# Two transformer blocks on one core: junctions, gates and the end of a recurrence rewritten together

## The chip, the cores and the metric

The kernel runs on one NeuronCore of a Trainium2 chip. The metric is the device time of one execution in microseconds; the kernel before has a median of 2291.05 us over three runs (2288.86 to 2294.74).

## What is computed

256 tokens of width 1024 go through a first block of two layers and a second block. Cut from the reference:

```
def first_block(x, ...):
    for layer in range(2):
        if layer == 0: mix = _diff_attention(x, ...)
        else:          mix = _stick_breaking(x, ...)          # keys and values from x too
        x = _layer_norm(ALPHA * x + mix, ln_g[layer, 0], ln_b[layer, 0])
        ffn = _peer(x, w_q, sub_keys, u, v)     # top 16 of 128 x 128 experts, 8 heads
        x = _layer_norm(ALPHA * x + ffn, ln_g[layer, 1], ln_b[layer, 1])

def rg_lru(x, w_a, b_a, w_i, b_i, lam):
    r = sigmoid(block_diag_linear(x, w_a, b_a))
    i = sigmoid(block_diag_linear(x, w_i, b_i))
    log_a = -8 * r * softplus(-lam)
    a = exp(log_a)
    bx = sqrt(-expm1(2 * log_a)) * (i * x)
    h = scan: h_t = a_t * h_(t-1) + bx_t

def second_block(x, ...):
    u = rms_norm(x, attn_pre_norm)
    q, k, v, x_lru, g_lru, gate_attn, gate_lru = split(u @ w_in)
    y_attn = moba_attention(q, k, v) @ w_branch_attn
    y_lru  = (rg_lru(conv(x_lru)) * gelu(g_lru)) @ w_branch_lru
    mix = (sigmoid(gate_attn) * y_attn + sigmoid(gate_lru) * y_lru) @ w_out
    h = x + rms_norm(mix, attn_post_norm)
    m = square(relu(rms_norm(h, mlp_pre_norm) @ w_up)) @ w_down
    return h + rms_norm(m, mlp_post_norm)
```

## The kernel before

The tokens lie in two halves of 128, b = 0 and b = 1. Every projection is done in split precision: a weight tile `raw` (128x1024) is cut by ScalarE into `hi` (`Stream.split`, L66) and by VectorE into `lo` = `raw` − `hi` (L67); so are the activations into `xh` and `xl` (`part`, L163 and L164); and three products hi·hi, lo·hi and hi·lo are added in a PSUM bank (`mm3`, L157 to L159, or `mm_n`, L182). All weights of the program pass through one `Stream` in the order of use. `next()` hands out a tile, issues the loads of the tiles three ahead on SP's queue, and cuts two ahead, or `extra` more; the cuts of the tiles named by `keep` go into buffers of their own. Each engine runs its instructions in the order in which the Python code issues them, so the place of a call in the code is its place in the engine's queue.

A stage ends in a *junction*: the last projection (`proj_n`, or the loop over the 128 row tiles of experts in `peer`) adds into four banks `ps_acc`, two for each half of the tokens. The products of the last `DEFER` = 6 tiles for b = 1 are held back (`held`), so that TensorE has them to do while the norm of b = 0 runs on VectorE and ScalarE. Then `layer_norm` norms b = 0 (`norm`, tiles `lny`, `lnm`, `lnr`, result `x` or `xr`), transposes it (`transposed`, bank `ps_m`, L289), multiplies it by the first `NJ` = 4 tiles of the next stage (`half_pass(0)`), and does the same for b = 1 (`half_pass(1)`). `half_pass(0)` takes its four tiles with `next()`, so the cuts that `next()` issues stand in the midst of it.

Block 2 norms by the root of the mean square. In `post_norm` ScalarE squares the banks with a sum (`msj`, `mss`, L910), VectorE scales (`qnu`) and adds to `x` (L944); `pre_norm` squares `x` again, scales by a gain (`pnu`) and by the root (L927, L928). Its mixer works on eight column tiles at a time: projections `gl`, `ga`, `gg` are copied from PSUM, `rr` and `ii` are Sigmoids of the block-diagonal products (L1163), and `ga` and `gl` are made Sigmoids later, 512 columns at a time (L1166). A generator in the background (`bg.tick()`) issues the attention heads and the recurrence: exponent `rr` times `decay`, `aa`, the factor under the root, the scans over `xc`, the Gelu of `gg`.

The tile `x` is spilled to DRAM (`xs`) between stages and read again when the next norm needs it.

## Time and profile before

| | |
|---|---|
| median of three runs | 2291.05 us (2288.86 to 2294.74) |
| profiled execution | 2293.14 us |
| its span in the profile | 2291.4 us |
| granted TensorE clock, mean | 0.991 |
| busy: TensorE, VectorE, ScalarE, GpSimd | 2224.8, 1744.0, 1238.1, 35.6 us |
| HBM | 437.39 MB read, 39.85 MB written |

The span is what the profile's rows cover; the profiled execution's own time is 1.7 us longer, and 2.1 us over the median. PE is TensorE, PEld its weight loads, DVE VectorE, ACT ScalarE, POOL GpSimd, SP SyncE; SPq and POOLq are DMA issues of these queues.

### The profile page before, as it was taken

What the parts mean: (1) busy time and instruction counts of PE and PEld (TensorE: products, weight loads), DVE (VectorE), ACT (ScalarE), POOL (GpSimd) and SP (SyncE); (2) the same over time, 40 slices, a digit from 0 to 9 for tenths busy, and PEclk for the clock granted to TensorE, in tenths of its full rate; (3) what the DMA queues carried; (4) which work ended last, traced back from release to release, by engine and by line L of the source; (5) the groups of instructions that cost most, each with busy time, mean ns of one, the idle gap of its engine ahead of it and who ended that gap; (6) DMA issues with size and microseconds to landing.
All of it is one profiled execution on the core that took longest, in us unless ns stands there. A gap on an engine that the chain in (4) does not pass through costs nothing.

```text
span 2291.4 us, 39855 instructions
## 1 busy us (share of the span) xinstructions
PE 2224.8 (97%) x15028; PEld 2007.0 (88%) x15028; DVE 1744.0 (76%) x3496; ACT 1238.1 (54%) x2128; POOL 35.6 (2%) x81
## 2 busy tenths in 40 slices
PE   8999999999999999999999999999999899998998
PEld 7779999999888887988999999888888689997987
DVE  6869999887666668577998988766667757676654
ACT  5644455666444444674445566544445447754543
POOL 4100000000000000000000000000000000000000
PEclk9999999999999999999999999999999999999999
DMA  7446676556777776554667665777877574464664
GB/s 251 153 171 229 217 239 222 199 197 234 241 243 260 241 243 215 170 169 166 230 225 235 211 205 190 244 243 240 262 240 254 171 214 141 145 215 154 204 192 140
DMA packets 152706, 481.96 MB, mean 210 GB/s; under 512 B 18752, under 2 KB 19648, under 8 KB 151232
## 3 DMA queue, kind: packets, MB, share of 16 engines
q1 hardware_dynamic: 131456, 442.69, 59.9%
q10 hardware_dynamic: 19008, 34.61, 4.0%
q8 instruction: 118, 1.93, 0.3%
q0 software_dynamic: 2048, 2.10, 0.3%
q14 instruction: 76, 0.62, 0.1%
HBM read 437.39 MB, written 39.85 MB: 208 GB/s over the span
## 4 chain that ended last, share of the span: by engine, by line
PE 87%; DVE 5%; ACT 4%; DMA 2%; issue 2%; POOL 0%; SPq 0%; DVEq 0%; ACTq 0%
PE ps_acc L182 35%; PE ps_h L157 15%; PE ps_h L159 15%; PE ps_h L158 14%; DVE lo L67 2%; PE ps_acc L807 1%; PE ps_acc L808 1%; ACT hi L66 1%; PE ps_acc L158 1%; PE ps_acc L157 1%; PE ps_acc L159 1%; DMA raw<-w_up 1%; PE ps_acc L691 0%; PE ps_m L289 0%; DVE lns L308 0%
## 5 line engine op out<-in xcount | busy, mean ns | idle before, releaser
L67 DVE TENSOR_TENSOR lo<-raw,hi 128x1024 fp32r<-128x1024 f32 x740 | 902.3, 1222 | 444.2 <-ACT hi L66 441.4
L66 ACT CAST hi<-raw 128x1024 fp32r<-128x1024 f32 x740 | 775.1, 1050 | 434.1 <-issue 308.5
L157 PE MATMUL ps_h<-xh,hi 128*128 128x256 f32 x2784 | 789.3, 284 | 3.7 <-ACT r L1239 2.2
L159 PE MATMUL ps_h<-xh,lo 128*128 128x256 f32 x2784 | 774.2, 278 | 1.5 <-DVE lo L67 1.4
L158 PE MATMUL ps_h<-xl,hi 128*128 128x256 f32 x2784 | 773.9, 278 | 0.0
L157 PEld LDWEIGHTS ps_h<-xh,hi 128*128 128x128 f32 x2784 | 525.9, 189 | 9.0 <-ACT r L1239 2.5
L159 PEld LDWEIGHTS ps_h<-xh,lo 128*128 128x128 f32 x2784 | 523.9, 188 | 2.8 <-DVE lo L67 2.5
L158 PEld LDWEIGHTS ps_h<-xl,hi 128*128 128x128 f32 x2784 | 524.4, 188 | 0.2
L182 PE MATMUL ps_acc<-hi,wh 128*128 128x512 f32 x1024 | 315.6, 389 | 3.3 <-ACT wh L163 3.3
L182 PE MATMUL ps_acc<-lo,wh 128*128 128x512 f32 x1024 | 315.2, 389 | 0.0
L182 PE MATMUL ps_acc<-hi,wo 128*128 128x512 f32 x1024 | 315.2, 389 | 0.0
L834 ACT ACTIVATE hs<-ps_h 128x256 f32<-128x256 f32 x256 | 98.3, 384 | 343.4 <-PE ps_h L159 173.0
L182 PEld LDWEIGHTS ps_acc<-hi,wh 128*128 128x128 f32 x1024 | 192.0, 188 | 43.5 <-ACT wh L163 3.6
L182 PEld LDWEIGHTS ps_acc<-lo,wh 128*128 128x128 f32 x1024 | 192.2, 188 | 40.0
L182 PEld LDWEIGHTS ps_acc<-hi,wo 128*128 128x128 f32 x1024 | 192.2, 188 | 39.8
L164 DVE TENSOR_TENSOR wo<-jd,wh 128x256 fp32r<-128x256 f32 x256 | 107.2, 419 | 2.0 <-ACT wh L163 2.0
L858 DVE TENSOR_TENSOR jd<-G,jd 128x256 f32<-128x256 f32 x256 | 107.0, 418 | 2.2 <-ACT G L810 2.2
L163 ACT CAST wh<-jd 128x256 fp32r<-128x256 f32 x256 | 101.7, 397 | 10.1 <-DVE jd L858 10.1
L810 ACT ACTIVATE G<-ps_acc 128x64 f32<-128x64 f32 (+1 forms) x256 | 82.1, 384 | 6.7 <-PE ps_acc L808 1.0
L157 PE MATMUL ps_h<-hi,xh 128*128 128x512 f32 x160 | 70.3, 439 | 13.1 <-ACT hi L66 11.0
L158 PE MATMUL ps_h<-lo,xh 128*128 128x512 f32 x160 | 68.3, 427 | 5.7 <-DVE lo L67 5.7
L159 PE MATMUL ps_h<-hi,xl 128*128 128x512 f32 x160 | 67.8, 423 | 2.0 <-DVE xl L164 2.0
(326 smaller groups left out, 2349.7 us busy)
## 6 DMA issues: line engine op xcount, KB each, us to landing
raw<-peer_u SPq DMA_DIRECT2D x256, 512.0 KB, 4.5
raw<-peer_v SPq DMA_DIRECT2D x256, 512.0 KB, 4.0
H<-hs SPq DMA_DIRECT2D x128, 256.0 KB, 2.1
jd<-H ACTq DMA_DIRECT2D x128, 256.0 KB, 3.9
raw<-w_in SPq DMA_DIRECT2D x32, 512.0 KB, 3.7
raw<-w_up SPq DMA_DIRECT2D x32, 512.0 KB, 3.8
raw<-w_down SPq DMA_DIRECT2D x32, 512.0 KB, 3.7
raw<-w_qkv SPq DMA_DIRECT2D x24, 512.0 KB, 4.5
```

What stands on the lines that cost most here:

```text
L66: self.nc.scalar.copy(hi, raw)
L67: self.nc.vector.tensor_sub(lo, raw, hi)
L157: mm(out, lh, rh, start=start, stop=False)
L158: mm(out, lh, rl, start=False, stop=False)
L159: mm(out, ll, rh, start=False, stop=stop)
L163: self.nc.scalar.copy(hi, src)
L164: self.nc.vector.tensor_sub(lo, src, hi)
L182: mm(acc[half], x, w[:, half * 512 : half * 512 + 512], start=a, stop=b)
L807: mm(out, o[:, 0, j], o[:, 1, j], start=True, stop=False)
L810: nc.scalar.activation(gt[:, :, 4 * g : 4 * g + 4], ps.rearrange("p (t i) -> p i t", t=4)[:, first:end], AF.Copy, scale=1.0 / GSCALE,)
L834: nc.scalar.activation(hs[i // 2][:, i % 2], o, AF.Gelu)
L858: nc.vector.tensor_tensor(w, g[:, i - first], hl[i // 2][:, i % 2], ALU.mult)
```

## The change

Seven edits come together. TensorE's list of products is as long as before; the order of some held products changes.

1. *Cuts.* `half_pass(0)` calls `next(calm=True)`, which cuts nothing ahead; the cuts that stood there are issued in `half_pass(1)`. All four junction tiles are cut before the norm: in `peer` by `extra` in the last iterations (two cuts more, at i = 119 and 120), elsewhere by a `split` ahead of `half_pass(0)`.
2. *Held products* run as half 0 (512 columns) of all six jobs and then half 1 (`finish`).
3. *`norm`:* the centring of the second 512 columns stands behind `x` of the first.
4. *Norms around the MLP:* `pre_norm` is left out. `u` = `x` · gain is formed at once for each 512 columns, and the root, which scales a row as a whole, is computed behind `half_pass(1)` (`late_norm`), squared into `factor`, and used in the last `post_norm`.
5. *35 DMAs* (spills, reloads, gains, masks, tables) are issued by POOL in place of SP.
6. *Gates:* `ga` and `gl` become Tanh at the copy from PSUM, `ii` Tanh, `rr` Exp; a sigmoid is (1 + tanh(z/2))/2 or 1/(1 + exp(−z)), the one folded into the operations behind it, the other by four VectorE RECIPROCALs of 128x512. Four activation table loads go, one is added; ScalarE has 2174 rows for 2183, VectorE 3155 for 3128.
7. *The recurrence's end* is issued in ten steps of one scan each, without the wait for all eight `gg`.

```
@@ class Stream
-    def next(self):
+    def next(self, calm=False):
-        self.split(i + 1 + self.split_ahead + self.extra, i)
+        self.split(i + 1 if calm else i + 1 + self.split_ahead + self.extra, i)
@@ finish, proj_n, half_pass
+    def finish(self, held):
+        for half in range(2):
+            for job in held:
+                self.mm_n(*job, (half,))
-            self.st.extra = max(0, min(2, NJ * (k + 2 - count + defer) // defer))
+            self.st.extra = max(0, min(2, k - count + 6))
-                tiles.append(self.st.next())
+                tiles.append(self.st.next(calm=True))
+            elif j:
+                self.st.split(self.st.used + j, self.st.used)
@@ norm
-        for s in halves:
-            nc.vector.scalar_tensor_tensor(y[:, s], y[:, s], mv[:, 0:1], g[:, s], ALU.subtract, ALU.mult)
+        centre = lambda s: nc.vector.scalar_tensor_tensor(y[:, s], y[:, s], mv[:, 0:1], g[:, s], ALU.subtract, ALU.mult)
+        centre(halves[0])
         next(root)
         for s in halves:
+            if s is halves[1]:
+                centre(s)
             nc.vector.scalar_tensor_tensor(x[:, b, s], y[:, s], r, beta[:, s], ALU.mult, ALU.add)
@@ layer_norm
+        self.st.split(self.st.used + NJ, self.st.used)
         next(n1)
         self.half_pass(0, tiles)
@@ peer
-                    nc.sync.dma_start(xr, spill)
+                    nc.gpsimd.dma_start(xr, spill)
+                if i >= GSPLIT:
+                    self.st.extra = min(2, (i - GSPLIT) // 4)
                 hi, lo = self.st.next()
@@ late_norm, post_norm
+    def late_norm(self, pool, x, square):
+        r = pool.tile([P, 1], F32, tag="lt_r", name=f"ltr{self.n}", bufs=2)
+        yield from self.mean_square(pool, r, [x[:, :512], x[:, 512:]], 1e-6)
+        self.nc.vector.tensor_tensor(square, r, r, ALU.mult)
             if out is not None:
                 nc.sync.dma_start(out[:, s], x[:, s])
+            if then:
+                then(s)
@@ block2, recurrence
+                nc.vector.reciprocal(decay, decay)
-                            nc.vector.tensor_scalar(rr[i][:, j], rr[i][:, j], d, None, ALU.mult)
+                            nc.vector.tensor_scalar(rr[i][:, j], rr[i][:, j], 1.0, d, ALU.add, ALU.mult)
+                        nc.vector.reciprocal(rr[i], rr[i])
-                while len(gelus) < KD:
-                    yield
-                for i in range(4 + 2):
+                for step in range(10):
+                    i, odd = divmod(step, 2)
...
+                            while len(gelus) < 2 * i + 2:
+                                yield
@@ block2, gates
-                        project(dst, c)
+                        nc.scalar.activation(dst[:, c], self.proj_t(self.xh, self.xl), AF.Tanh, scale=0.5)
-                nc.scalar.preload_act_table(AF.Sigmoid)
-                            nc.scalar.activation(d, o, AF.Sigmoid, bias=cv[:, c, 5 + i : 6 + i])
-                for g in (ga, gl):
-                    for c in range(half * 4, half * 4 + 4, 2):
-                        nc.scalar.activation(g[:, c : c + 2], g[:, c : c + 2], AF.Sigmoid)
+                            if dst is rr:
+                                nc.scalar.activation(d, o, AF.Exp, scale=-1.0, bias=gb[:, c, 0:1])
+                            else:
+                                nc.scalar.activation(d, o, AF.Tanh, scale=0.5, bias=gb[:, c, 1:2])
-                nc.vector.tensor_tensor(ya[:, c], o, ga[:, c], ALU.mult)
+                nc.vector.scalar_tensor_tensor(ya[:, c], ga[:, c], 1.0, o, ALU.add, ALU.mult)
@@ block2, junction
-                self.post_norm(two, acc[b], x[:, b], gains[0])
-                u = self.pre_norm(two, x[:, b], gains[1])
+                u = two.tile([P, D], F32, tag="ln_y", name=f"lnu{b}", bufs=2)
+                scaled = lambda s: nc.vector.tensor_tensor(u[:, s], x[:, b, s], gains[1][:, s], ALU.mult)
+                self.post_norm(two, acc[b], x[:, b], gains[0], then=scaled)
             self.half_pass(1, tiles)
-            nc.sync.dma_start(spill, x)
+            for b in range(NB):
+                for _ in self.late_norm(two, x[:, b], factor[:, b : b + 1]):
+                    pass
+            nc.gpsimd.dma_start(spill, x)
@@ MLP
-            nc.sync.dma_start(x, spill)
+            nc.gpsimd.dma_start(x, spill)
-                self.post_norm(two, acc[b], x[:, b], gain, a["out"][b * P : b * P + P])
+                self.post_norm(two, acc[b], x[:, b], gain, a["out"][b * P : b * P + P], factor[:, b : b + 1])
```

VectorE at peer 0's junction, the end of the norm of b = 1 (`lny`, `lnr`, `xr`) up to the split of its transposed values (`xl`), before:

```order
L264 TENSOR_TENSOR lnr_10685<-rsy_10706,rsz_10707 128x1
L316 SCALAR_TENSOR_TENSOR xr_9153<-lny_10682,lnr_10685,gains_10290 128x512 x2
L67 TENSOR_TENSOR lo_10722<-raw_10608,hi_10721 128x1024
L67 TENSOR_TENSOR lo_10734<-raw_10719,hi_10733 128x1024
L67 TENSOR_TENSOR lo_10746<-raw_10731,hi_10745 128x1024
L67 TENSOR_TENSOR lo_10758<-raw_10743,hi_10757 128x1024
L164 TENSOR_TENSOR xl<-ps_m_10767,xh 128x4x128
L164 TENSOR_TENSOR xl<-ps_m_10774,xh 128x4x128
```

The same place after the change:

```order
L273 TENSOR_TENSOR lnr_10695<-rsy_10716,rsz_10717 128x1
L329 SCALAR_TENSOR_TENSOR xr_9153<-lny_10692,lnr_10695,gains_10290 128x512
L323 SCALAR_TENSOR_TENSOR lny_10692<-lny_10692,lnm_10694,gains_10290 128x512
L329 SCALAR_TENSOR_TENSOR xr_9153<-lny_10692,lnr_10695,gains_10290 128x512
L164 TENSOR_TENSOR xl<-ps_m_10759,xh 128x4x128
L164 TENSOR_TENSOR xl<-ps_m_10766,xh 128x4x128
L67 TENSOR_TENSOR lo_10781<-raw_10735,hi_10780 128x1024
L67 TENSOR_TENSOR lo_10791<-raw_10743,hi_10790 128x1024
L67 TENSOR_TENSOR lo_10801<-raw_10751,hi_10800 128x1024
```

The four cuts `lo` stood between the norm and `xl`; now three stand behind `xl`, and the junction's other two are among the rows of the loop.

ScalarE at the junction behind the mixer, from the transposed values of b = 0 (`xh`) to those of b = 1, before:

```order
L163 CAST xh<-ps_m_24260 128x4x128
L163 CAST xh<-ps_m_24267 128x4x128
L66 CAST hi_24291<-raw_24281 128x1024
L66 CAST hi_24303<-raw_24289 128x1024
L910 ACTIVATE msj_24315,mss_24316<-ps_acc_24064 128x512
L910 ACTIVATE msj_24315,mss_24316<-ps_acc_24065 128x512
L258 ACTIVATE rsy_24323<-mss_24316,eps1e-06_76 128x1
L259 ACTIVATE rsy_24323<-rsy_24323 128x1
L910 ACTIVATE msj_24335,mss_24336<-x_23763 128x512 x2
L258 ACTIVATE rsy_24342<-mss_24336,eps1e-06_76 128x1
L259 ACTIVATE rsy_24342<-rsy_24342 128x1
L928 ACTIVATE pnu_24334<-pnu_24334,pnr_24333 128x512
```

The same place after the change:

```order
L163 CAST xh<-ps_m_24245 128x4x128
L163 CAST xh<-ps_m_24252 128x4x128
L927 ACTIVATE msj_24293,mss_24294<-ps_acc_24066 128x512
L927 ACTIVATE msj_24293,mss_24294<-ps_acc_24067 128x512
L266 ACTIVATE rsy_24301<-mss_24294,eps1e-06_76 128x1
L267 ACTIVATE rsy_24301<-rsy_24301 128x1
L163 CAST xh<-ps_m_24313 128x4x128
L163 CAST xh<-ps_m_24320 128x4x128
```

The two `hi` ahead of the Squares of b = 1 and the second root are gone from between the two transpositions.

VectorE in the mixer around the second pair of `rr` (exponents of the recurrence; `su` and `p` belong to an attention head), before:

```order
L164 TENSOR_TENSOR cl_22549<-xc_21398,ch_22548 128x256
L1076 TENSOR_SCALAR rr_21389<-rr_21389,decay_21912 128x256 x2
L1081 TENSOR_TENSOR ii_21397<-ii_21397,xc_21398 128x512
L1039 RECIPROCAL su_22541<-su_22541 128x2
L1041 TENSOR_SCALAR p_22539<-p_22539,su_22541 128x128
```

The same place after the change:

```order
L164 TENSOR_TENSOR cl_22553<-xc_21406,ch_22552 128x256
L1108 TENSOR_SCALAR rr_21397<-rr_21397,decay_21919 128x256 x2
L1109 RECIPROCAL rr_21397<-rr_21397 128x512
L1114 SCALAR_TENSOR_TENSOR ii_21405<-ii_21405,xc_21406 128x512
L1070 RECIPROCAL su_22545<-su_22545 128x2
L1072 TENSOR_SCALAR p_22543<-p_22543,su_22545 128x128
```

A RECIPROCAL of 512 columns stands ahead of the head's `su` and `p`.

## Rows read from the trace of the kernel before

**Rows 1.** The page's first part, busy time, share of the span and instructions of each engine, and a line of its fourth part, the share of each engine in the chain of work that ended last.

```profile
PE 2224.8 (97%) x15028; PEld 2007.0 (88%) x15028; DVE 1744.0 (76%) x3496; ACT 1238.1 (54%) x2128; POOL 35.6 (2%) x81
...
PE 87%; DVE 5%; ACT 4%; DMA 2%; issue 2%; POOL 0%; SPq 0%; DVEq 0%; ACTq 0%
```

**Rows 2.** Windows over the whole span; of each stretch from:to (us) its length, then busy time (and instructions) of each engine, then the granted TensorE clock, the busy share of the DMA engines, and GB/s. The stretches are the ends of layer 0, peer 0, peer 1, the mixer of block 2, and the kernel.

```profile
99.00:145.00 46.00, 40.79 (x172) 31.00 (x170) 34.54 (x62) 24.34 (x49) 0.00 (x0) 0.94 0.37 126
...
904.00:922.00 18.00, 13.65 (x48) 10.05 (x48) 11.73 (x19) 5.84 (x9) 0.00 (x0) 0.81 0.40 125
...
1782.00:1835.00 53.00, 45.56 (x187) 35.31 (x187) 39.66 (x76) 25.71 (x45) 0.14 (x2) 0.94 0.44 149
...
2066.00:2110.00 44.00, 36.16 (x145) 28.19 (x144) 28.78 (x51) 24.70 (x44) 0.00 (x0) 0.88 0.39 137
...
2284.00:2291.40 7.40, 0.00 (x0) 0.00 (x0) 3.55 (x9) 1.19 (x5) 0.00 (x0) 0.62 0.19 71
```

**Rows 3.** The timeline of peer 0's junction; columns are start, duration, engine, line, operation, out<-in, count, and in brackets the idle time ahead and what ended it.

```profile
903.30 0.51 PE L157 MATMUL ps_h<-hi,xh 128*128 128x512 f32 x1 [0.24 <-ACT xh L163]
...
904.37 0.40 PE L157 MATMUL ps_h<-hi,xh 128*128 128x512 f32 x1
...
906.24 0.40 PE L159 MATMUL ps_h<-hi,xl 128*128 128x512 f32 x1
...
907.07 3.87 ACT L66 CAST hi<-raw 128x1024 fp32r<-128x1024 f32 x4
...
908.66 1.42 DVE L316 SCALAR_TENSOR_TENSOR xr<-lny,lnr,gains 128x512 f32<-128x512 f32 x2
909.99 4.62 DVE L67 TENSOR_TENSOR lo<-raw,hi 128x1024 fp32r<-128x1024 f32 x4
...
911.26 0.80 PE L158 MATMUL ps_h<-lo,xh 128*128 128x512 f32 x1 [2.61 <-DVE lo L67]
...
917.86 0.50 PE L157 MATMUL ps_h<-hi,xh 128*128 128x512 f32 x1 [0.22 <-ACT xh L163]
```

**Rows 4.** The timeline of the ends of layer 0 (first three rows) and layer 1 (last row), columns as above.

```profile
128.29 1.40 DVE L313 SCALAR_TENSOR_TENSOR lny<-lny,lnm,gains 128x512 f32<-128x512 f32 x2
...
131.05 1.53 PE L289 MATMUL ps_m<-ident,x 128*128 128x128 f32 x8 [2.93 <-DVE x L316]
...
142.09 0.50 PE L159 MATMUL ps_h<-hi,xl 128*128 128x512 f32 x1 [0.62 <-DVE xl L164]
...
1045.77 0.50 PE L159 MATMUL ps_h<-hi,xl 128*128 128x512 f32 x1 [1.40 <-DVE xl L164]
```

**Rows 5.** The timeline of peer 1's junction, VectorE, columns as above.

```profile
1797.91 1.23 DVE L67 TENSOR_TENSOR lo<-raw,hi 128x1024 fp32r<-128x1024 f32 x1 [0.32 <-ACT hi L66]
...
1816.18 4.62 DVE L67 TENSOR_TENSOR lo<-raw,hi 128x1024 fp32r<-128x1024 f32 x4
```

**Rows 6.** The timeline of the junction behind the mixer of block 2, columns as above.

```profile
2082.50 0.59 ACT L910 ACTIVATE msj<-ps_acc 128x512 f32<-128x512 f32 x1
...
2086.36 1.42 DVE L944 SCALAR_TENSOR_TENSOR x<-qnu,qnr,x 128x512 f32<-128x512 f32 x2
...
2087.69 0.69 DVE L923 TENSOR_TENSOR pnu<-x,gains 128x512 f32<-128x512 f32 x1
...
2090.69 1.45 PE L289 MATMUL ps_m<-ident,pnu 128*128 128x128 f32 x8 [3.83 <-DVE pnu L927]
...
2092.66 2.00 ACT L66 CAST hi<-raw 128x1024 fp32r<-128x1024 f32 x2
...
2103.02 1.94 PE L289 MATMUL ps_m<-ident,pnu 128*128 128x128 f32 x8 [3.93 <-DVE pnu L927]
...
2104.78 0.80 PE L157 MATMUL ps_h<-hi,xh 128*128 128x512 f32 x1
```

**Rows 7.** The timeline of the MLP's first tiles, SP's queue, ScalarE and TensorE, columns as above.

```profile
2113.23 2.21 SPq L50 DMA_DIRECT2D raw<-w_up  x4
...
2121.86 1.04 ACT L66 CAST hi<-raw 128x1024 fp32r<-128x1024 f32 x1 [6.46 <-DMA raw<-w_up]
...
2123.55 0.39 PE L157 MATMUL ps_h<-xh,hi 128*128 128x256 f32 x1 [2.25 <-ACT r L1239]
```

**Rows 8.** The timeline of the kernel's end, ScalarE, columns as above.

```profile
2283.32 0.60 ACT L910 ACTIVATE msj<-ps_acc 128x512 f32<-128x512 f32 x1 [5.40 <-PE ps_acc L182]
```

**Rows 9.** Windows over the mixer's gates and recurrence (columns as in group 2), then VectorE's reciprocals by line and shape (count, busy us, mean ns, idle time ahead), and a timeline row of POOL's queue.

```profile
1929.00:1946.00 17.00, 14.47 (x117) 13.80 (x115) 7.77 (x16) 15.05 (x30) 0.10 (x1) 1.00 0.39 124
1946.00:1961.00 15.00, 15.00 (x125) 14.74 (x124) 13.46 (x29) 12.43 (x30) 0.10 (x1) 1.00 0.43 124
...
1981.00:1994.00 13.00, 11.55 (x92) 10.95 (x91) 3.58 (x5) 11.04 (x20) 0.00 (x0) 1.00 0.40 123
1994.00:2005.00 11.00, 9.05 (x73) 8.50 (x72) 9.64 (x14) 10.00 (x18) 0.00 (x0) 1.00 0.42 132
...
2014.00:2036.00 22.00, 18.71 (x153) 18.19 (x152) 20.05 (x31) 12.63 (x17) 0.00 (x0) 1.00 0.50 155
...
L1039 DVE RECIPROCAL su<-su 128x2 f32<-128x2 f32 x8 | 1.3, 158 | 0.0
...
L735 DVE RECIPROCAL gsum<-gsum 128x8 f32<-128x8 f32 x4 | 0.8, 204 | 0.1
...
45.55 1.96 POOL L420 DMA_DIRECT2D zsk<-zk  x4 [0.76 <-ACT zk L417]
```

More of the change, by code (lines that the diff above doesn't have):

```diff
@@ L175, in proj_t, with mm_n @@
         return o
-    def mm_n(self, acc, xh, xl, hi, lo, start, stop):
+    def mm_n(self, acc, xh, xl, hi, lo, start, stop, halves=range(2)):
         mm = self.nc.tensor.matmul
         for x, w, a, b in ((xh, hi, start, False), (xh, lo, False, False), (xl, hi, False, stop)):
-            for half in range(2):
+            for half in halves:
                 mm(acc[half], x, w[:, half * 512 : half * 512 + 512], start=a, stop=b)
+    def finish(self, held):
+        for half in range(2):
+            for job in held:
+                self.mm_n(*job, (half,))
     def proj_n(self, xh, xl, count, pool, defer, ready=None):
@@ L204, in proj_n @@
         self.st.extra = 0
-        for job in held:
-            self.mm_n(*job)
+        self.finish(held)
         return acc
@@ L892, in peer @@
                         held.append(job)
-            for job in held:
-                self.mm_n(*job)
+            self.st.extra = 0
+            self.finish(held)
             vctx.close()
@@ L929, in pre_norm, with post_norm @@
         return u
-    def post_norm(self, pool, acc, x, gain, out=None):
+    def late_norm(self, pool, x, square):
[3 more added lines that the diff above has]
+        yield
+    def post_norm(self, pool, acc, x, gain, out=None, by=None, then=None):
         nc = self.nc
@@ L970, in block2 @@
         mm = nc.tensor.matmul
-        outer = ExitStack()
+        outer, ctx_f = ExitStack(), ExitStack()
+        fp = ctx_f.enter_context(tc.tile_pool(name="b2f", bufs=1))
+        factor = fp.tile([P, NB], F32, tag="factor", name="factor")
         keep = outer.enter_context(tc.tile_pool(name="b2o", bufs=1))
```

84 lines of the change are left out of this document (47 added, 37 removed).

## The prediction

> **What bounds the kernel now.** I read the page's totals and chain first: TensorE is busy 2224.8 us of the span and is 87% of the chain that ended last [rows 1]. The change leaves TensorE's list of products as long as it was, so what can be won is TensorE's idle time (2291.4 − 2224.8 = 66.6 us) and whatever runs at the lower clock. Next the windows, to place it: five stretches leave TensorE idle for 46.00 − 40.79 = 5.2, 4.35, 7.4, 7.8 and, behind the last product, 7.4 us, and in all five the granted clock is under 1 [rows 2]. These are the ends of layer 0, peer 0, peer 1, the mixer, and the kernel. Then the timeline of each stretch, where the reader is to see who is awaited.
>
> **Peer 0's junction.** `half_pass(0)` starts at 903.30 and halts twice for its third tile, once for the cast `hi` and up to 911.26 for its `lo` (2.61 us; the window has 4.35 in all), and the granted clock over the window is 0.81 [rows 2, 3]. The casts are late because only two of the four tiles were cut earlier: four `hi` stand in one row at 907.07 and four `lo` at 909.99 behind the norm of the second tokens [rows 3]. Now all four are cut in the loop (`extra` in its last iterations) and the next stage's cuts move into `half_pass(1)`. A pass that runs unhindered I estimate at 5.6 us (from 904.37 to 906.24 eight products follow at 0.234 us each, and a pass has 24): `half_pass(0)` would end at 908.9. `xr` of the second tokens comes at 908.66 and no longer has the `lo`s behind it, so its first half is ready near 909.4 and `half_pass(1)` starts another 1.4 us later (at the lower clock 1.76, from 2103.02 to 2104.78 in the mixer [rows 6]), at 910.8 and not at 917.86: −7.0. Against it, two more `lo` (1.2 each) stand ahead of the first norm on VectorE, which covers them only in part: I take back 1.0. **−6.0** (bounds −7.1 and −3.5).
>
> **Layer 0 and layer 1.** The first transposition waits 2.93 us for `x`; putting the second half's centring (0.7, half of the row of two at 1.40) behind `x` of the first half brings it 0.7 forward, twice in a junction. The two `lo` that the next stage's cuts put ahead of `xl` move behind it: the waits of 0.62 and 1.40 us fall away [rows 4]. With a part of the low-clock time **−2.0 each, −4.0** (bounds −2 and −6).
>
> **Peer 1's junction** has the same four `lo`, but here the first norm is on the path: VectorE's last `lo` runs from 1797.91 to 1799.1, and `lny` follows it at once. Two more `lo` push it back by up to 2.4, what the removed block of four (4.62 at 1816.18) gives back to the second norm is 4.62 less the squares and small steps that stood behind it in any case [rows 5]: about −2.6 + 2.4 and 0.7 for the centring. **−1.0** (bounds −4.5 and +1.5).
>
> **The mixer's junction.** Before, `x` of the first tokens stands at 2086.36, but then come `pnu`, two Squares on it, a root, and a multiplication; the transposition starts only at 2090.69, after 3.83 us of waiting, and that of the second tokens at 2103.02 after 3.93 [rows 6]. In the new text the order on VectorE is x, u, x, u: the second u is ready 0.72 + 0.69 + 0.72 + 0.69 = 2.8 us behind 2086.36, the first at 2087.8; `half_pass(0)` starts near 2089.0. ScalarE's row of two `hi` at 2092.66 (2.00 us) leaves its place ahead of the second tokens' Squares, which now stand right behind the `xh` casts: I place them at 2090.3, x 3.1 to 3.9 later as in the first tokens' chain (2082.50 to 2086.36), the second transposition at 2094.8 to 2096, and `half_pass(1)` near 2097.3 where it was 2104.78 [rows 6]. **−7.5** (bounds −9 and −5). The root that was taken out comes back as `late_norm` behind `half_pass(1)`: four Squares at about 0.6 and two roots, an estimated 5 us of ScalarE in front of the first Relu. TensorE has two banks of `ps_h` to write (2.8 us each) while they run, so I cost it at nothing; without that cover it is up to 3 us.
>
> **Start of the MLP.** The loads of `w_up` are issued at 2113.23, behind the reload of `x` and the `gain` on SP's queue. The cast `hi` at 2121.86 has waited 6.46 us for them, the Relu stands behind it on ScalarE, and TensorE waits 2.25 us for that Relu's bank up to 2123.55 [rows 7]. Those two go to POOL's queue. **−2.5** with the clock behind the wait (bounds −4 and +3, the Relu above). **End:** of the two Squares behind the last product (0.60 each, the first at 2283.32) one is now covered, since the first half ends six jobs earlier: **−0.7** [rows 8].
>
> **Gates and reciprocals.** Four table loads of ScalarE go and one comes. TensorE idles 2.5 us in 1929 to 1946, 1.45 in 1981 to 1994 and 1.95 in 1994 to 2005, most of it for these loads and the Sigmoids on whose banks TensorE waits: I count −4.4 of the 5.9. Against this, VectorE gets four RECIPROCALs of 512 columns. No row has this shape: 2 columns take 158 ns and 8 take 204, so by slope (7.7 ns a column) 158 + 510 × 7.7 = 4.1 us; had they the rate of a usual 512-column operation it would be 0.7 (`pnu`, 0.69) [rows 6, 9]. I take 4.1: the slope is of the same instruction. VectorE has 9.2 us free in the first and 9.4 in the third window, but 1.5 and 1.4 in the second and the fourth [rows 9]; the first and third reciprocal are hidden, the second and the fourth stand ahead of `lo` casts that TensorE needs: 4.1 − 1.5 and 4.1 − 1.4 = 5.3, and the operations that already stood in the way make it, say, 6.4. Sum **+2.0** (bounds −4.4, reciprocals free, and 16.4 − 4.4 = +12). VectorE: DVE Perf Modes of the Trainium skill (section Walkthrough: the 8-slice pipeline in each mode) says that a reciprocal runs as an iterated divide on two slices of the pipe with a repeat count of 8. No run here shows it yet; the slope of 7.7 ns a column against 1.3 for `pnu` (0.69 us by 512) is a factor of 6, which bears the rule out so far.
>
> **Recurrence's end.** From 2014 to 2036 VectorE is busy 20.05 of 22 us and TensorE idles 3.3 [rows 9]; the first scans no longer wait for all eight gates and use the free time before 2014. **−1.5** (bounds −3.3 and +1).
>
> **DMAs moved to POOL.** 35 loads and spills leave SP's queue; four issues took 2.21 there [rows 7], so 35 by 0.55 are 19 us of a queue that mostly waits: worth nothing outside the MLP's start. A POOL issue takes about 0.5 us (four in 1.96) [rows 9]. I cost them at nothing, since they are issued in the stage ahead of the one that reads them; without that cover each would cost what its transfer is late. DMA: Bandwidth & Descriptors in the Trainium skill (section SWDGE vs HWDGE vs iDMA) says that descriptors for POOL's transfers are written by software into SBUF, from which VectorE can lock it out, and that plain transfers belong on SP or ScalarE; by it these loads would come late by an amount that no row here gives.
>
> **Sum.** −6.0 − 4.0 − 1.0 − 7.5 − 2.5 − 0.7 + 2.0 − 1.5 = −21.2 us. The profiled execution took 2293.14 (span 2291.4), 2.1 over the median of 2291.05, so I apply the difference to the median: 2291.05 − 21.2 = **2269.9 us**.
>
> **Rivals.**
> - *Junctions' gains are mostly eaten:* the extra `lo`s delay the first norms fully (2.4 at both peers), the clock drops in the gaps that remain, as it did at 0.81 in peer 0's window. Then peer 0 gives −3.5, the layers −2, peer 1 +1.5, the mixer −5: −9 with the rest at −2.7, so about 2279. For it: VectorE's tightness at 1797.91. Chance 0.15.
> - *Reciprocals cost little:* at 0.7 us the gates give −4.4 and the sum is −27.6: 2263.5. Against it the slope. Chance 0.15.
> - *Reciprocals decide (other side):* all four exposed and each a second time, since the attention's softmax rows stand behind them and TensorE waits for its transpositions: 4 × 4.1 × 2 − 4.4 = +28, which is over the 23.2 of the other terms: 2296. It decides once a reciprocal costs the path more than (23.2 + 4.4)/4 = 6.9 us. Against it the 9 us free in two of the windows. Chance 0.04.
> - *POOL's transfers late:* `x`, `gain` or the spill hold the Relu, or a norm waits for its gains. Ten places with about 2 us each (a POOL transfer's four issues) would give −1: 2290, no measurable change. Chance 0.08.
>
> **Numbers.** The forecast (2263 to 2277) has 0.58. The range 2257 to 2284 takes in the first two rivals and the bounds of the reciprocals; outside lie the last two and some of the tails. What a measurement of this kernel can tell from no change is about 0.3%, 6.9 us: faster means under 2284. Faster 0.86, same 0.09, slower 0.05.
>
> **What would show it.** In the profile after: no `hi` and `lo` waits inside `half_pass(0)` of both peers, a granted clock near 1 in 904 to 922; the transposition of the mixer's junction some 3 us earlier; RECIPROCAL 128x512 near 4 us with TensorE waiting for `lo` behind the second and fourth; no idle time of 2 us behind the first `w_up` tiles. Wrong it would be if the first norms start later by more than the cuts saved, if a TensorE wait ends with a POOL transfer, or if VectorE's total rises by much more than 17 us.

## The result and the profile after

The changed kernel takes 2265.56 us (median of 5, 2264.94 to 2268.64) against 2291.43 for the kernel before in the same session; the ratio is 0.9889 with a 95% interval of 0.9876 to 0.9903, so 25.9 us or 1.1% less. Forecast were 2269.9 us (−21.2) and a range of 2257 to 2284. The profiled execution took 2268.64 us, the slowest of the five; its span is 2266.5, 24.9 less than before's.

The page's totals and the chain by engine, which answer to [rows 1]:

```profile
PE 2218.0 (98%) x15028; PEld 2000.1 (88%) x15028; DVE 1757.2 (78%) x3501; ACT 1229.8 (54%) x2115; POOL 54.8 (2%) x118
...
PE 85%; DVE 5%; issue 4%; ACT 3%; DMA 3%; POOL 0%; ACTq 0%; DVEq 0%; SPq 0%; POOLq 0%
```

TensorE is idle for 2266.5 − 2218.0 = 48.5 us instead of 66.6: 18 of the 25 us are idle time. The rest, 6.8 us of busy time, goes in the main with the granted clock, whose mean rose from 0.991 to 0.995; smaller parts of both signs, in which equal products run at another pace at a clock of 1.00, are told in the last section. Windows over the same five stretches, moved with the work (columns as in [rows 2]); the last begins where the last product ends:

```profile
99.00:142.00 43.00, 39.66 (x171) 29.79 (x171) 34.59 (x63) 24.67 (x49) 0.54 (x1) 0.97 0.44 148
902.00:916.00 14.00, 13.28 (x64) 10.15 (x62) 12.14 (x20) 6.07 (x10) 0.97 (x2) 1.00 0.28 101
...
1774.00:1825.00 51.00, 45.59 (x183) 35.24 (x182) 40.55 (x75) 25.98 (x45) 2.01 (x4) 0.90 0.53 183
...
2050.00:2088.00 38.00, 34.18 (x145) 26.59 (x144) 27.32 (x39) 19.73 (x31) 0.54 (x1) 0.96 0.49 170
...
2258.80:2266.50 7.70, 0.00 (x0) 0.00 (x0) 2.92 (x8) 1.27 (x4) 0.00 (x0) 0.75 0.18 68
```

Idle time in the first four is now 3.3, 0.7, 5.4 and 3.8 us where 5.2, 4.35, 7.4 and 7.8 stood, and the clock is at 1.00 in peer 0's junction, though in peer 1's it is lower than before (0.90 for 0.94). The fifth, behind the last product, has shortened little: 2266.50 − 2258.87 = 7.6 us from the last product to the end, for 2291.40 − 2283.32 = 8.1 before. To see where each microsecond went I set the starts of the same events in both traces side by side; a step is the difference less that of the line above.

| event | before, us | after, us | difference | step | what lies in the step |
|---|---|---|---|---|---|
| first `hs` of peer 0 | 164.30 | 161.13 | −3.17 | −3.17 | layer 0's junction |
| first `wh` of peer 0 | 553.24 | 550.95 | −2.29 | +0.88 | no edit that shows: kernels alike here take 388.4 to 389.8 us |
| end of the 2.1 us wait in layer 1's attention | 1004.95 | 998.36 | −6.59 | −4.30 | peer 0's junction |
| first `hs` of peer 1 | 1066.86 | 1058.49 | −8.37 | −1.78 | layer 1's junction |
| first `wh` of peer 1 | 1458.00 | 1449.62 | −8.38 | −0.01 | |
| first wait for a bank of `rr` | 1930.12 | 1919.68 | −10.44 | −2.06 | peer 1's junction |
| wait for the `lo` of a `gg` tile | 2011.17 | 1998.75 | −12.42 | −1.98 | gates and reciprocals |
| end of the mixer's held products | 2086.86 | 2070.49 | −16.37 | −3.95 | recurrence's end |
| start of `half_pass(1)` in the mixer | 2104.78 | 2083.49 | −21.29 | −4.92 | the mixer's junction |
| last Relu of the MLP | 2196.52 | 2169.73 | −26.79 | −5.50 | rest of it, start of the MLP |
| end of the last product | 2283.32 | 2258.87 | −24.45 | +2.34 | the MLP's second projection |
| end of the span | 2291.40 | 2266.50 | −24.90 | −0.45 | the kernel's end |

### The profile page after: what moved, and what is told of

Its sections match the earlier page's. It is cut to its first block, busy times and chain, and to the rows that moved or that the text cites. A ratio compares the mean times of both kernels' runs of the same rounds, so it can differ in the third digit from the quotient of the medians.

```text
span 2266.5 us, 39922 instructions
## 1 busy us (share of the span) xinstructions
PE 2218.0 (98%) x15028; PEld 2000.1 (88%) x15028; DVE 1757.2 (78%) x3501; ACT 1229.8 (54%) x2115; POOL 54.8 (2%) x118
## 4 chain that ended last, share of the span: by engine, by line
PE 85%; DVE 5%; issue 4%; ACT 3%; DMA 3%; POOL 0%; ACTq 0%; DVEq 0%; SPq 0%; POOLq 0%
PE ps_acc L182 31%; PE ps_h L157 15%; PE ps_h L159 15%; PE ps_h L158 15%; DVE lo L67 1%; PE ps_acc L821 1%; PE ps_acc L822 1%; PE ps_acc L157 1%; PE ps_acc L158 1%; PE ps_acc L159 1%; ACT hi L66 1%; DMA raw<-peer_v 1%; PE ps_acc L705 0%; DMA raw<-peer_w_q 0%; DVE lns L319 0%
## 5 line engine op out<-in xcount | busy, mean ns | idle before, releaser
L821 PE MATMUL ps_acc<-oh 128*128 128x128 f16 x512 | 69.6, 221 | 0.0
L822 PE MATMUL ps_acc<-oh 128*128 128x128 f16 x512 | 68.6, 219 | 0.0
```

The source lines that it names most:

```text
L821: mm(out, o[:, 0, j], o[:, 1, j], start=True, stop=False)
L822: mm(out, o[:, 0, j], o[:, 2, j], start=False, stop=True)
```

## Experiments

Each kernel is the changed one with one edit undone or altered, unless it says otherwise. All ratios are to the kernel before in the same session, so the changed kernel's 0.9889 (0.9876 to 0.9903) is the number to hold against; 0.001 is 2.3 us. A median of one session and that of another differ by some us for the kernel before alone (2290.43 to 2292.52), so ratios are compared, not medians.

### Gates as before

```
-                        nc.vector.reciprocal(rr[i], rr[i])
...
-                        nc.scalar.activation(dst[:, c], self.proj_t(self.xh, self.xl), AF.Tanh, scale=0.5)
+                        project(dst, c)
...
+                nc.scalar.preload_act_table(AF.Sigmoid)
...
+                            nc.scalar.activation(d, o, AF.Sigmoid, bias=cv[:, c, 5 + i : 6 + i])
...
```

> The changed kernel with the gates as before: Sigmoids with their table loads, no reciprocals; all else stays changed. Changed kernel: 2265.6 us. My theory (the gates' gain and the reciprocals nearly cancel; between the landmarks that stood at 1929 and 2014 us TensorE gained 1.8 us): 2266 to 2269, with TensorE idle again by 2.2 and 1.1 us behind two table loads and no idle time behind reciprocals. Rival A, the gates pay and the reciprocals are nearly hidden: 2270 or more. Rival B, the reciprocals cost more than the Sigmoids did: 2264 or less.

Measured: ratio 0.9891 (0.9873 to 0.991), 2267.44 us. The timeline of this kernel, ScalarE's table load ahead of the second half's gates and TensorE behind it:

```profile
1966.78 1.28 ACT L1182 ACT_TABLE_LOAD   x1
...
1969.55 0.39 PE L157 MATMUL ps_h<-ch,hi 128*128 128x256 f32 x1 [1.11 <-ACT rr L1195]
```

The old waits are back (2.20 us behind the first half's table load, 1.11 behind this one), those behind reciprocals gone, and the time is the same within the interval, as expected. Edit 6 as made is worth nothing that these runs can tell: what it frees on ScalarE it spends on VectorE.

### `rr` as a Tanh, no reciprocals

```
-                nc.vector.tensor_scalar(decay, decay, -8.0, None, ALU.mult)
-                nc.vector.reciprocal(decay, decay)
+                nc.vector.tensor_scalar(decay, decay, -4.0, None, ALU.mult)
...
-                        nc.vector.reciprocal(rr[i], rr[i])
...
-                                nc.scalar.activation(d, o, AF.Exp, scale=-1.0, bias=gb[:, c, 0:1])
+                                nc.scalar.activation(d, o, AF.Tanh, scale=0.5, bias=gb[:, c, 0:1])
```

(`gb` holds half the bias in place of its negative.) The exponent is (1 + tanh(z/2)) · decay with half the decay, so no division is left.

> The changed kernel with rr as a Tanh too (sigmoid as half of 1 + tanh, the factor 4 times softplus in place of 8), so that the four reciprocals of 512 columns and the one of 8 fall away. My theory: the idle times of 1.58 us (attention's transposition behind the second reciprocal) and 2.78 us (a lo cast behind the fourth) go, 4.4 us in all: 2260 to 2263. Rival: those waits are taken over by what stands behind them (hi casts on ScalarE, the attention's chain): 2264.5 to 2266.

Measured: ratio 0.9856 (0.9837 to 0.9876), 2258.24 us: better than both kernels, as are the two that are built on it below (0.9857 and 0.9861), and better than the 2260 to 2263 that I expected. First the changed kernel's timeline around the second and the fourth reciprocal, VectorE and TensorE:

```profile
1935.66 3.35 DVE L1109 RECIPROCAL rr<-rr 128x512 f32<-128x512 f32 x1
...
1943.08 0.55 PE L1079 MATMUL ps_m<-ident,p 128*128 128x128 f32 x3 [1.58 <-DVE al L164]
...
1981.91 3.35 DVE L1109 RECIPROCAL rr<-rr 128x512 f32<-128x512 f32 x1
1986.32 1.22 DVE L67 TENSOR_TENSOR lo<-raw,hi 128x1024 fp32r<-128x1024 f32 x1
1987.59 0.38 PE L159 MATMUL ps_h<-xh,lo 128*128 128x256 f32 x1 [2.78 <-DVE lo L67]
```

And windows of the Tanh kernel over the places where these stood:

```profile
1930.00:1946.00 16.00, 16.00 (x136) 15.75 (x135) 13.48 (x34) 11.73 (x27) 1.69 (x4) 1.00 0.63 200
...
1974.00:1984.00 10.00, 10.00 (x87) 10.00 (x86) 9.51 (x13) 8.31 (x14) 0.00 (x0) 1.00 0.58 164
```

TensorE is idle for 0 us in both. Between the wait for `rr` (1919.68 after, 1915.13 here) and that for `gg`'s `lo` (1998.75, 1990.17) the Tanh kernel gains 8.58 − 4.55 = 4.0 us: the two waits, 1.58 + 2.78 = 4.4. The other 4.5 us of the two profiles lie ahead of the gates, where the programs are alike; they are the spread of executions (last section), the changed kernel's profile being its slowest and this one its fastest. By the medians the gain is 0.0033 or 7.6 us; a gain of 4 us lies within the intervals, and what would be more than that is not explained.

### The 35 DMAs on SP again

```
-            nc.gpsimd.dma_start(x, spill)
+            nc.sync.dma_start(x, spill)
...
```

> The changed kernel with the 35 DMAs issued by SP again, the rest changed. My theory: only the start of the MLP is lost, 2.5 to 4 us, and TensorE waits about 2 us behind its first tiles again: 2268 to 2270. Rival A, POOL's transfers come late somewhere and cost: 2264 or less. Rival B, the moved DMAs are worth nothing anywhere, since with the cuts moved too the loads stand early enough: 2265 to 2267.

Measured: ratio 0.9922 (0.9906 to 0.9937), 2275.60 us: 0.0033 or 7.6 us slower than the changed kernel, nearly twice the 4.4 that I expected at most. The timeline at the start of the MLP, SP's queue, ScalarE and TensorE:

```profile
2096.50 0.33 SPq L1259 DMA_DIRECT2D x<-xs  x1
2096.87 0.42 SPq L281 DMA_DIRECT2D gain<-mlp_post_norm  x1
2097.34 9.88 SPq L50 DMA_DIRECT2D raw<-w_up  x5
2104.57 1.04 ACT L66 CAST hi<-raw 128x1024 fp32r<-128x1024 f32 x1 [8.56 <-DMA raw<-w_up]
...
2106.25 0.58 PE L157 MATMUL ps_h<-xh,hi 128*128 128x256 f32 x1 [6.31 <-ACT r L1278]
```

The row of the kernel before had 2.25 in place of 6.31 [rows 7]. The reload of `x` on SP comes only when `late_norm` has read the old `x` (SP's wait of 12.3 us ahead of it ends with `factor`), and the loads of `w_up` stand behind it; the granted clock is 0.50 from 2105.2 to 2112.0. Whether that is the reason, the kernel with this edit and the root's both undone tells, further down.

### Cuts as before

```
-            self.st.extra = max(0, min(2, k - count + 6))
+            self.st.extra = max(0, min(2, NJ * (k + 2 - count + defer) // defer))
...
-                tiles.append(self.st.next(calm=True))
-            elif j:
-                self.st.split(self.st.used + j, self.st.used)
+                tiles.append(self.st.next())
...
-        self.st.split(self.st.used + NJ, self.st.used)
...
-                if i >= GSPLIT:
-                    self.st.extra = min(2, (i - GSPLIT) // 4)
```

> The changed kernel with the cuts as before: half_pass(0) cuts ahead, no extra cuts in the peers' loops, none ahead of half_pass(0). The order inside the norm and of the held products, the norms around the MLP, DMAs, gates and recurrence stay changed. My theory (the cuts are what held peer 0, and half of the other junctions' gain): peer 0 loses 4 to 5, peer 1 1 to 2, the layers 2 together, the mixer 1: 2274 to 2276, with the 2.61 us waits for lo inside half_pass(0) back. Rival, the order inside the norm and of the held products made most of it: 2267 to 2270.

Measured: ratio 0.9944 (0.9928 to 0.9959), 2278.96 us: 0.0055 or 12.6 us, the largest single part and more than I gave it. The timeline of its peer 0 junction, where the rows of [rows 3] return:

```profile
907.63 3.87 ACT L66 CAST hi<-raw 128x1024 fp32r<-128x1024 f32 x4
908.72 0.50 PE L157 MATMUL ps_h<-hi,xh 128*128 128x512 f32 x1 [1.53 <-ACT hi L66]
910.67 3.49 DVE L67 TENSOR_TENSOR lo<-raw,hi 128x1024 fp32r<-128x1024 f32 x3
911.95 0.79 PE L158 MATMUL ps_h<-lo,xh 128*128 128x512 f32 x1 [2.73 <-DVE lo L67]
```

And at the ends of layer 0 and layer 1, where the waits for `xl` of [rows 4] return, longer than they were (0.62 and 1.40):

```profile
142.13 0.50 PE L159 MATMUL ps_h<-hi,xl 128*128 128x512 f32 x1 [1.68 <-DVE xl L164]
...
1043.62 0.51 PE L159 MATMUL ps_h<-hi,xl 128*128 128x512 f32 x1 [1.68 <-DVE xl L164]
```

### No extra cuts in the peers' loops

```
-                if i >= GSPLIT:
-                    self.st.extra = min(2, (i - GSPLIT) // 4)
```

> The changed kernel without the extra cuts in the peers' last loop iterations, so that two of the four junction tiles are cut by the split ahead of half_pass(0); the next stage's cuts stay in half_pass(1). Changed kernel: 2265.6 us. In its trace the last tiles of both peers' loops come 2.7 to 3.4 us later than in the kernel before, which I put down to the extra cuts. My theory: at peer 0 the extra cuts pay (half_pass(0) would wait for its third tile), at peer 1, where the first norm is on the path, they cost as much as they save: 2266 to 2269. Rival, the price at the loops' ends outweighs the gain in both: 2262 to 2264.5.

Measured: ratio 0.9889 (0.9874 to 0.9903), 2267.63 us: no difference from the changed kernel, in the expected range. The timeline at peer 1's transpositions, without the extra cuts:

```profile
1799.51 1.09 PE L300 MATMUL ps_m<-ident,pnu 128*128 128x128 f32 x8 [0.87 <-DVE pnu L942]
...
1812.99 1.30 PE L300 MATMUL ps_m<-ident,pnu 128*128 128x128 f32 x5 [6.03 <-DVE pnu L942]
```

and of the changed kernel at the same place:

```profile
1802.69 1.97 PE L300 MATMUL ps_m<-ident,pnu 128*128 128x128 f32 x8 [2.97 <-DVE pnu L944]
...
1814.35 1.07 PE L300 MATMUL ps_m<-ident,pnu 128*128 128x128 f32 x8 [2.12 <-DVE pnu L944]
```

What the first transposition gains, the second loses. The loop's end does move: the seventh `wh` from the end starts 0.9 us earlier without the extra cuts and the third from the end 3.05. At peer 0 my theory fell: `half_pass(0)` does not wait for its third tile there, TensorE waits 1.73 and 0.82 us at the second transposition instead (0.48 in the changed kernel). So it is not where the two extra cuts stand that cost the kernel with the cuts as before; the calm `half_pass(0)` and the `split` ahead of it are left, which were not undone one by one.

### The recurrence's end as before

```
-                for step in range(10):
+                while len(gelus) < KD:
+                    yield
+                for i in range(4 + 2):
```

> The changed kernel with the recurrence's end as before (steps of pairs, behind all eight gg), the gates as changed. Between the landmarks at 2014 and 2036 us TensorE gained 3.9 us by the change. My theory: that is this edit, 2268.5 to 2270. Rival, the gain came from the reciprocals' and gates' move, which leaves VectorE freer there: 2265 to 2267.

Measured: ratio 0.9912 (0.9899 to 0.9924), 2272.66 us: 0.0023 or 5.3 us slower, more than expected, though the intervals just overlap. Two rows of its timeline:

```profile
2013.30 0.36 PE L157 MATMUL ps_h<-ah,hi 128*128 128x256 f32 x1 [1.46 <-ACT hi L66]
...
2017.87 0.36 PE L157 MATMUL ps_h<-ah,hi 128*128 128x256 f32 x1 [1.45 <-ACT hi L66]
```

Both waits stood in the kernel before and neither in the changed one, whose window over these products has TensorE busy throughout:

```profile
2002.00:2021.00 19.00, 19.00 (x161) 18.97 (x160) 18.80 (x28) 10.74 (x15) 0.00 (x0) 1.00 0.66 188
```

That is 2.9 us by rows; the whole step of the table takes 75.9 us in this kernel's profile, 75.7 in the kernel before's and 71.7 in the changed one's. The gain belongs to this edit, not to the gates.

### The root in front of the MLP again

```
-                self.post_norm(two, acc[b], x[:, b], gains[0], then=scaled)
+                self.post_norm(two, acc[b], x[:, b], gains[0])
+                u = self.pre_norm(two, x[:, b], gains[1])
...
-                for _ in self.late_norm(two, x[:, b], factor[:, b : b + 1]):
-                    pass
```

> The changed kernel with the root of the mean square in front of the MLP's first transposition again (pre_norm, no late_norm), the moved DMAs and cuts as changed. The junction behind the mixer gained 6.3 us in the trace. My theory: most of that is this edit: 2270 to 2272, with waits of some 3 us ahead of both transpositions. Rival, the cuts and the order of the Squares gave it: 2266 to 2268.

Measured: ratio 0.9906 (0.9891 to 0.9921), 2272.69 us: 0.0017 or 3.9 us slower, with intervals that overlap. The timeline says more; the two transpositions here:

```profile
2076.72 1.78 PE L300 MATMUL ps_m<-ident,pnu 128*128 128x128 f32 x8 [4.59 <-DVE pnu L944]
...
2087.13 1.89 PE L300 MATMUL ps_m<-ident,pnu 128*128 128x128 f32 x8 [2.01 <-DVE pnu L944]
```

and in the changed kernel, with VectorE's rows ahead of the first:

```profile
2071.58 0.75 DVE L968 SCALAR_TENSOR_TENSOR x<-qnu,qnr,x 128x512 f32<-128x512 f32 x1
2072.37 0.69 DVE L1238 TENSOR_TENSOR lnu<-x,gains 128x512 f32<-128x512 f32 x1
...
2073.11 0.66 PE L300 MATMUL ps_m<-ident,lnu 128*128 128x128 f32 x4 [2.62 <-DVE lnu L1238]
...
2074.59 0.81 PE L300 MATMUL ps_m<-ident,lnu 128*128 128x128 f32 x4 [0.82 <-DVE lnu L1238]
...
2082.21 1.04 PE L300 MATMUL ps_m<-ident,lnu 128*128 128x128 f32 x8
```

The wait of 4.59 + 2.01 becomes 2.62 + 0.82 + 0: 3.2 us by idle time.

### The orders inside the norm and of the held products as before

```
-        centre(halves[0])
+        centre(halves[0])
+        centre(halves[1])
...
-        for half in range(2):
-            for job in held:
-                self.mm_n(*job, (half,))
+        for job in held:
+            self.mm_n(*job)
```

> The changed kernel with the second half's centring ahead of x again and the held products job by job (edits 2 and 3 undone). My theory: 0.7 us at each of four layer norms of the first tokens where TensorE waits for x, and 0.7 at the kernel's end: 2267.5 to 2270. Rival, these orders are hidden behind the held products: 2265 to 2267.

Measured: ratio 0.9884 (0.987 to 0.9898), 2267.01 us: not to be told from the changed kernel. In its trace TensorE waits 1.81 us once for layer 0's first transposition, against 1.36 and 0.79 in two pieces; 0.7 us a place was too much. At the kernel's end it is 0.5 us longer behind the last product, as the order of the held products would have it. Inconclusive beyond that.

### Root in front and DMAs on SP together

> The changed kernel with two edits undone together: pre_norm ahead of the MLP again (no late_norm), and the 35 DMAs on SP again. Undone alone, the first gave 2272.7 us (+7.1) and the second 2275.6 (+10.0). In the second, SP's reload of x waits until late_norm has read the old x and holds the loads of w_up behind it (TensorE waits 6.31 us). My theory: without late_norm that wait is short, so the DMAs are worth only 2 to 4 us here: 2274 to 2278. Rival, the two edits are independent and add: 2281 to 2284.

Measured: ratio 0.9924 (0.991 to 0.9939), 2274.92 us. Against the kernel with the root in front alone (0.9906) the DMAs cost 0.0018; against the changed kernel they cost 0.0033. If the two edits added, 0.9906 + 0.0033 = 0.9939 would have been measured, which is the interval's edge, so the time alone leaves it open. The timeline decides:

```profile
2102.30 1.04 ACT L66 CAST hi<-raw 128x1024 fp32r<-128x1024 f32 x1 [6.70 <-DMA raw<-w_up]
...
2103.99 0.39 PE L157 MATMUL ps_h<-xh,hi 128*128 128x256 f32 x1 [2.28 <-ACT r L1274]
```

TensorE waits 2.28 us, as in the kernel before, not 6.31. Moving the reload to POOL takes away a wait of 2.3 us if the root stays in front, and one of 6.3 us and a clock drop if it moves behind.

With these two taken together the parts add up: 0.0055 for the cuts, 0.0023 for the recurrence's end and 0.0035 for root and DMAs are 0.0113, where the whole change is 0.0111; gates and orders are nothing that can be told. Undone alone, root and DMAs make 0.0017 and 0.0033, which would be 0.0050.

### The kernel before with only the DMAs moved

> The kernel before with nothing changed but the queue of the 35 DMAs, POOL in place of SP. Kernel before: about 2292 us. My theory: it loses TensorE's wait at the MLP's start (2.25 us and the low clock behind it) and gains a wait of about 1 us at the start of layer 1 for tri_in: 2288 to 2291. Rival A, the DMAs are worth as much as in the changed kernel (10 us): 2280 to 2284. Rival B, software transfers cost more than they free: above 2293.

Measured: ratio 0.9981 (0.9971 to 0.9992), 2288.56 us, 4.3 us less than the kernel before, in the expected range. In its trace no wait of TensorE is left at the MLP's start. The other half of the expectation failed: there is no wait for `tri_in` at the start of layer 1. The transfer lands at 922.58, and the cast of `tri` comes at 924.22 behind ScalarE's own work. With the cuts as before that transfer is early enough; it is late only when the junction ahead of it is faster.

### A late cast of `tri`

```
-            nc.scalar.copy(tri, tri_in)
...
+                if c == 0:
+                    nc.scalar.copy(tri, tri_in)
```

(with the Tanh). The changed kernel waits at layer 1's start, ScalarE and TensorE:

```profile
916.10 0.54 POOL L564 DMA_DIRECT2D tri_in<-c_tri  x1
...
922.07 0.41 ACT L565 CAST tri<-tri_in 128x256 fp32r<-128x256 f32 x1 [3.77 <-DMA tri_in<-c_tri]
...
922.80 0.38 PE L157 MATMUL ps_h<-xh,hi 128*128 128x256 f32 x1 [0.98 <-ACT k L628]
```

> The changed kernel with rr as a Tanh without reciprocals (2258.2 us alone) and the cast of tri, which stood at the head of ScalarE's queue in layer 1 and waited 3.77 us for the transfer of tri_in, put behind the first k and q. My theory: the idle time of 0.98 to 1.41 us of TensorE at the start of layer 1 goes: 2256.5 to 2257.5, which these rounds can hardly tell from 2258.2, so the verdict is by the trace. Rival, something else waits there in its place (the first k behind another transfer): the idle time stays.

Measured: ratio 0.9857 (0.984 to 0.9874), 2258.17 us: the wait is gone from the trace (`tri` at 920.39 waits 0.21 us), and the time cannot tell it.

### A longer tile ahead of block 2

```
-        factor = fp.tile([P, NB], F32, tag="factor", name="factor")
+        factor = fp.tile([P, 16], F32, tag="factor", name="factor")[:, :NB]
```

> The kernel with rr as a Tanh and the late cast of tri (2258.2 us), and the tile factor (8 bytes in a partition) made 64 bytes long, nothing else. In all kernels with edit 4 the 384 products of the MLP's second projection take 88.9 us from the first start to the last, in the kernel before and in that with only the DMAs moved 86.9; the rows of one product are 394 ns long for 389. The allocation that differs is factor, which lies ahead of block 2's tiles: uh lies at byte 82656 of a partition after, 82624 before, that is 32 bytes off a multiple of 64. My theory: the place of the operands makes the difference, so with factor at 64 bytes (uh at 82688) the projection takes 86.9 us again and the kernel 2 us less: 2255.5 to 2257. Rival, the order of products or the norm's new place in the code makes it: 88.9 us and 2258.

Measured: ratio 0.9861 (0.9842 to 0.9879), 2259.25 us, and the 384 products take 88.9 us as in the changed kernel. The theory fell for this stage. (The kernels with the root in front, without edit 4, keep the tile `factor` and take 88.9 us too.) By line and shape, TensorE in the second projection, in the kernel before and then in this one (count, busy us, mean ns of one):

```profile
L182 PE MATMUL ps_acc<-lo,uh 128*128 128x512 f32 x128 | 39.4, 389 | 0.0
```

```profile
L182 PE MATMUL ps_acc<-lo,uh 128*128 128x512 f32 x128 | 41.1, 394 | 0.0
```

But the tile's length is not without effect. Windows over the same 190 products of the mixer, in the same order, in the kernel with the late cast and then in this one, which differ in that length alone (PE with the products that reach into the window, clock, DMA share, GB/s):

```profile
1939.12:1961.50 22.38, 22.38 (x193) 1.00 0.69 244
```

```profile
1941.40:1964.36 22.96, 22.96 (x193) 1.00 0.73 241
```

All kernels with the tile at 8 bytes take 22.38 us there, and the two without it, the kernel before and that with only the DMAs moved, 22.83.

## Why the prediction was right, by its steps

The direction, the range and the likeliest case (2263 to 2277) held. The terms, against the steps of the table:

- **Peer 0, −6.0: came out at −4.3.** The mechanism holds: `half_pass(0)` no longer stops, and `half_pass(1)` starts at 910.44 where I placed it at 910.8. Two terms were small. The loop's end comes late, so `half_pass(0)` starts 0.3 us before the old 903.30 though the stage began 2.3 ahead: 2.0 against the 1.0 that I took back, 1.45 of it in the last eight iterations. And `tri_in` adds 0.98 behind it.
- **Layers, −4.0: −3.2 and −1.8, together −5.0.** The kernel with the old orders cannot be told from the changed one, so the 0.7 us of centring was not the cause that I made it. The kernel with the cuts as before shows that the moved cuts are: its first `hs` of peer 0 comes at 164.33, as in the kernel before (164.30), and from the wait in layer 1's attention to the first `hs` of peer 1 it takes 60.3 us, where the four kernels with moved cuts whose clock is at 1.00 there, as its own is, take 58.5 to 58.6.
- **Peer 1, −1.0: −2.1.** Inside the bounds. Its first transposition waits longer than before (2.97 for 1.22 us) and its second is earlier, which is what the forecast's two opposite terms say. The size is not firm: from the first `wh` of peer 1 to the first `rr` the kernels with moved cuts take 469.8 to 472.3 us, the kernel before 473.8.
- **Mixer and MLP's start, −7.5 and −2.5: −4.9 and −5.5, −10.4 for −10.0 together.** The first transposition came 1.2 us sooner behind the held products (2.62 for 3.83), not 3, because the Squares of the first tokens came late: the cast `hi` ahead of them waited 3.04 us for `w_up`. The second is larger: the trace shows no wait at all after `half_pass(1)`, `late_norm` was hidden as I costed it, and the clock, of which I said only that it came with the wait, made the rest: over the 25.2 us from the start of `half_pass(1)` it was 0.86 before and is 1.00. ScalarE in the changed kernel:

```profile
2066.78 1.05 ACT L66 CAST hi<-raw 128x1024 fp32r<-128x1024 f32 x1 [3.04 <-DMA raw<-w_up]
2067.73 0.59 ACT L927 ACTIVATE msj<-ps_acc 128x512 f32<-128x512 f32 x1
```

- **Gates and reciprocals, +2.0: the step is −2.0, but only −0.1 of it is the term.** Between the two landmarks the idle time that stood there fell from 5.9 to 1.4 us, 4.5 where I counted 4.4. A reciprocal takes 3354 ns, not 4100, and the two that I named are the two that stall TensorE, by 1.58 + 2.78 = 4.4 us where I said 6.4 (the second by way of the attention's transposition, not of a weight's cast). So the term came out 2.1 us below the forecast, and the time of the kernel with the gates as before agrees that it is near nothing. The other 1.8 us of the step are no idle time: the same 608 products, in the same order at a clock of 1.00, are busy 73.3 us for 75.1. The kernel with the gates as before has the new pace too (22.38 us for the 190 products of the last experiment), so it is not this edit. VectorE: DVE Perf Modes of the Trainium skill (section Walkthrough: the 8-slice pipeline in each mode) names the iterated divide; the trace agrees with a price of its own kind: 3354 ns against 684 for a plain operation of the same size, a factor of 5.
- **Recurrence, −1.5: −3.95.** I gave it half of the idle time there; of the step 3.0 us are idle time (3.65 fell to 0.62), the rest is pace. The kernel with it undone has two of the waits back.
- **DMAs, nothing beyond the MLP's start: right by the kernel with the DMAs alone (−4.3), wrong in one place,** the transfer of `tri_in`, which takes 5.7 us from POOL where 2.3 stood on SP, and starts after the spill has landed. That is the rival of late POOL transfers, at 1 us and not at 20. DMA: Bandwidth & Descriptors of the Trainium skill (section SWDGE vs HWDGE vs iDMA) gives SP's path the faster setup and would keep plain transfers there. The trace agrees for the reloads, `x<-xs` takes 7.3 us from issue to landing for 5.7 before, and not for the spills, `xs<-x` 4.1 for 4.2. It does not decide here, since what costs is a transfer that waits at the head of SP's queue.
- **End, −0.7: −0.45.** The second Square alone stands behind the last product, as said.
- **Not foreseen: +2.3 in the MLP's second projection** (below), the 1.8 us of pace in the gates' stretch, and +0.9 in peer 0's first products, which is within the spread of executions.

The rivals: that the reciprocals cost little (2263.5) fell by their 3354 ns and the two stalls, though its time is nearer to the 2265.56 than the forecast's; that the junctions' gains are eaten fell by 10.4 and 4.3. The sum was 3.7 us off the difference of the spans (−21.2 for −24.9; 2269.9 − 2265.56 = 4.3 by the medians), with errors of up to 3 us in single terms. That the sum is no further off is in part luck: the start of the MLP (−5.5 for −2.5) and the recurrence (−3.95 for −1.5) were undersized, while the mixer (−4.9 for −7.5) was oversized and the MLP's second projection gave 2.3 back. The 4.4 us of the two stalls are what the Tanh kernel wins.

## What to carry to other kernels

Cuts, casts and loads that belong to the next stage stand in every engine's queue where the code issues them, and the cheapest gain is to move them behind the work that TensorE is about to need. Price a moved load by the wait at the head of its queue in the new program, not in the old: the same move was worth 0.0018 of the time (4.1 us, a wait of 2.3 in it) with the root in front and 0.0033 (7.6 us, a wait of 6.3 in it) with it behind. And before a function is replaced by a reciprocal, look whether another form needs none: the Tanh of half the argument gave the gates' gain (ratio 0.9856, 0.9837 to 0.9876) without the two stalls.

## What the runs showed of the hardware that I had not expected

The same 384 products in the MLP's second projection take 86.9 us in the kernel before and in the one with only the DMAs moved, and 88.9 us in the changed kernel and all the others, at a granted clock of 1.00 and with no idle time: 389 against 394 ns a product. Windows of equal length, early and late in the projection, in the kernel before and then in the changed one (the instructions on `ps_acc` alone: PE, PEld, VectorE, ScalarE; then clock, DMA share, GB/s):

```profile
2210.00:2230.00 20.00, 20.00 (x90) 16.57 (x89) 0.00 (x0) 0.00 (x0) 1.00 0.69 191
2268.00:2282.00 14.00, 14.00 (x64) 11.58 (x63) 1.38 (x2) 1.38 (x4) 1.00 0.11 39
```

```profile
2180.00:2200.00 20.00, 20.00 (x87) 16.12 (x86) 0.00 (x0) 0.00 (x0) 1.00 0.65 195
2244.00:2258.00 14.00, 14.00 (x64) 11.58 (x63) 2.08 (x3) 2.33 (x6) 1.00 0.11 39
```

The slower pace, 233 ns from start to start for 227, holds for the first 26 of the 32 tiles, in which products of both halves of the tokens alternate and weights still arrive. Within ten products of the place from which those of b = 1 are held back all kernels run at 227. It is not the order of the held products, the cuts, the root, the DMAs, the gates or the recurrence, since kernels with each undone show it, and not the 32 bytes by which `factor` moved the tile `uh`: at 64 bytes, it stayed. What all the slower kernels share and the two faster ones lack is, among other things, two small tiles that the change adds, `factor` and `gb`; no kernel was run without them, so the cause is open, and with it 2 us. That `factor`'s length can change the pace of equal products at all is shown in the mixer by the last experiment (22.38 us for 22.96, one profile of each).

Elsewhere single stretches of equal products differ between the executions too: the profiled Tanh kernel was 4.5 us ahead of the changed one before the gates, where the programs are the same. 1.6 of these lie between the wait in layer 1's attention and the first `hs` of peer 1, where the granted clock fell in one execution and not in the other. The changed kernel and then the Tanh kernel (PE, clock, DMA share, GB/s):

```profile
990.00:1020.00 30.00, 27.91 (x131) 0.94 0.45 148
```

```profile
988.50:1018.50 30.00, 27.90 (x138) 1.00 0.50 161
```

Another 1.8 lie in the two stretches from the first `hs` to the first `wh` of a peer, which took 389.8 and 391.1 us for 388.9 and 390.2 with no lower clock in either. A difference of one profile below some 5 us is read from the waits, not from the span.
